# Delta rule output gates: projected with channels on the partitions, applied behind the transposes

## The chip, the core and the metric

The kernel runs on one core of a Trainium2 chip. The metric is the device time of one execution in microseconds; the time of a kernel is the median of its runs. The engines are TensorE (PE, matmuls and weight loads), VectorE (DVE), ScalarE (ACT), GpSimd (POOL) and SyncE (SP, which issues most of the DMAs). Each works through its own queue in order.

## What is computed

One layer of a decoder: a SwiGLU block, a mixer, a second SwiGLU block, a final RMS norm, for 512 tokens of 1024 channels in float32. The mixer has an HGRN2 branch and a gated delta rule branch of 16 value heads. The part at issue is the end of the delta rule branch: its output is normed per head, gated with `silu(gz)`, and projected.

```
proj = (u @ w_in).astype(f32)
(hq, hf, hi, hg, gq, gk, gv, ga, gb, gz, gate_h, gate_g) = jnp.split(proj, offsets, axis=-1)
...
o_g = gated_delta_chunked(q_g, k_g, v_g, beta, g)              # 16 heads of 128 channels
o_g = rmsnorm(o_g, gdn_out_norm) * silu(gz).reshape(B, S, 16, 128)
y_g = o_g.reshape(B, S, 2048) @ w_branch_gdn
y = sigmoid(gate_h) * y_h + sigmoid(gate_g) * y_g
```

## The kernel before

A float32 product is made of three fp32r matmuls: each operand is split into a high part (an ACT cast) and a low part (a DVE difference). `mm3` (L165) issues the three, on lines L166 to L168. A weight slab of 128x512 is loaded by SP into one of 3 `raw` tiles and split into one of 6 `whi` and `wlo` tiles, which are used in turn (`RB`, `WB`). `uh` and `ul` hold the split, normed input with channels on the partitions; the factor of each token's RMS norm is applied to the result, either by `rbc` (along the free axis) or by `rcol` (one per partition).

The mixer is one list schedule written at build time. Every piece of work is a generator that asks for an engine with an estimated duration, for tiles (`get`) and for events (`on`); the class `Desk` runs these in simulated time and so writes the order of all queues. A long line of dense projections (`DENSE`, then sixteen merge gates t0 to t15) is worked through by `product` as a filler between the pieces of the recurrences. In `DENSE`, `k`, `q`, `v` are the delta rule's projections, `y` the first branch's output, and `z0` to `z7` the output gates, each for two heads (a unit `u`).

A `z` projection (L1911 to L1933) has tokens on the partitions: per block of 128 tokens the stationary operand is `uh` or `ul`, and 256 weight columns move, 8 contraction steps of three matmuls for each of 4 token blocks. Two blocks share a PSUM bank (`mm`, 2 banks in all). `gate` (L1619) makes of each 128x256 half `(tanh(z r / 2) + 1) z` with ACT (L1624) and DVE (L1626) in a tile of `gz`; the bank is then given back.

The recurrence of a unit is `g_rec` (L1454). Per chunk, PE makes `pks`, `pw` and `pog`; ACT copies `pw` to `w` (L1465), which `pog` needs. After the last chunk POOL takes the power -1/2 of the mean squares (L1551) and multiplies by `rcol` (L1552); DVE makes the gated output `on` of each 128x128 block, output times `rho` times gate (L1560); PE transposes four blocks into a bank `b` (L1568, `pto`); ACT evicts that with the norm's gain (L1583); SP writes the head to DRAM (`keep`, L1587). For the last unit the transposed output goes straight into the split operand (L1575, L1577).

The close: `tgate` (L1596) multiplies a merge gate by `rbc` (L1601), takes tanh (L1604) and SP writes it out; each holds one of six `ta` tiles until the write has landed, t15 stays on chip. `operand` (L1634) loads a head back into a `ta` tile (`og`, L1643) and splits it (L1649, L1651); heads that go into `uh` and `ul` wait for the end of the projections. `merged` (L1664) loads three tiles for each output tile (`mi`, `mt`, `mg`), of which `mg` holds a `ta` tile. `closing` (L1700) makes the branch products, four slabs of four heads (twelve matmuls) each; the first two products take turns, slab by slab, so the order is first slab of the first, first slab of the second, and so on. A product needs a PSUM bank of the two `mm`, the second one that of t15.

Of the kernel before, what the change touches and what calls it, by code (L numbers as in the profile page):

```python
# [8 lines left out]
F32 = mybir.dt.float32  # L9
# [3 lines left out]
ALU = mybir.AluOpType  # L13
# [19 lines left out]

DENSE = (
# [3 lines left out]
)  # L38
MERGE = (None, None, "a", "a", "b", "b", None, None)
LATE = 1  # L40
# [776 lines left out]
def mixer(tc, mp, e):  # L817
# [636 lines left out]
    def g_rec(u, st):  # L1454
# [84 lines left out]
                D.fire(("s", u, c))  # L1539
        D.put("s")  # L1540
        D.fire(("K", u))
        yield "on", ("norm", u, 1), ("z", u), *[("o", u, c) for c in range(NT)]
        ss, rho, gz = sm[:, 5], sm[:, 6], G["gz"][u % 3]

        yield "use", "DVE", .4
# [4 lines left out]
        yield "use", "POOL", 2.2  # L1550
        pool.tensor_tensor(rho, rho, mhalf[:, :8], op=ALU.pow)  # L1551
        pool.tensor_tensor(v3(rho, 2), v3(rho, 2), mid(rcol, 2), op=ALU.mult)  # L1552
        yield "lag", EASE
        ons = []
        for i in range(2):
            yield "get", "on", 1
            ons.append(places["on"]("on", (P, NT, P)))
            for c in range(NT):
                yield V(200)
                dve.scalar_tensor_tensor(ons[i][:, c], at[i][:, c], rho[:, 4 * i + c:4 * i + c + 1],  # L1560
                                         gz[:, c, i * P:(i + 1) * P], op0=ALU.mult, op1=ALU.mult)
        D.fire(("R", u))
        for i in range(2):
            yield "get", "b", 1
            yield T_(.5)
            pt = ps("pto", "b")
            for c in range(NT):
                pe.transpose(pt[:, c * P:(c + 1) * P], ons[i][:, c], ident)  # L1568
            if u == 7:
                yield "on", "projected"  # L1570
                yield A(560)
                k = 14 + i
                a, b = so[k] = uh[:, k - 8], ul[:, k - 8]
                gn = cs[:, C_GN:C_GN + 1]
                act.activation(a, pt, AF.Copy, scale=gn)  # L1575
                yield V(560)
                dve.scalar_tensor_tensor(b, pt, gn, a.bitcast(F32), op0=ALU.mult, op1=ALU.subtract)  # L1577
                D.put("b")
                D.fire(("so", k))
                continue  # L1580
            og = ons[i].rearrange("p c b -> p (c b)")
            yield A(512)
            act.activation(og, pt, AF.Copy, scale=cs[:, C_GN:C_GN + 1])  # L1583
            D.put("b")
# [11 lines left out]
    def tgate(i, pt):  # L1596

        yield "get", "ta", 1
        yield *V(512), 1
        g = ta("tg")  # L1600
        dve.tensor_tensor(g, pt, rbc, op=ALU.mult)  # L1601
        D.put("mm")
        yield A(512)
        act.activation(g, g, AF.Tanh, scale=0.5)  # L1604
        if i in stay:
            stay[i] = g
            D.fire(("t", i))
# [146 lines left out]
    def more():  # L1754
        yield "on", "branch", ("qm", 1)
        G["kq"].append(ex(0, P, NT, 2, P))
        G["gz"].append(ex(1, P, NT, 256))
# [21 lines left out]
    def weights(k, i):  # L1779
        if k == "B":  # L1780
            return [wn[2 * i + q // 4][:, q % 4 * 512:q % 4 * 512 + 512] for q in range(8)]
        if k == "z":
            return [wn[8 + i][:, q * 512:(q + 1) * 512] for q in range(4)]
        if k == "D":
            return [wab]
        src = wbh[i] if k == "y" else wt[{"Q": 0, "F": 8, "q": 16, "k": 24, "v": 32, "t": 48}[k] + i]
        return [src[:, q * 512:(q + 1) * 512] for q in range(2)]

    def choose():
        under = sum(("f", x) in D.at and x not in D.at for x in convs)  # L1790
        for x in todo:
            k, i = x
            need = {"Q": [("pd", i - 2)] if i > 1 else [], "F": [("L", i - 4)] if i > 3 else [],
                    "B": [("pair", i - 2)] if i > 1 else [], "D": [],
                    "y": [("O", 5), ("S", 6), ("S", 7)], "z": [("R", i - 3)] if i > 2 else [("gz", i) if i < 2 else "more"],
                    "v": [("K", i // 2 - 3)] if i > 5 else [("vb", i) if i < 4 else "more"],
                    "q": [("I", i - 4)] if i > 3 else ["decays" if i < 3 else "more"],
                    "k": [("I", i - 4)] if i > 3 else ["decays" if i < 3 else "more"]}[k]
# [74 lines left out]
    def product():  # L1873
        for n in range(len(todo) + len(gates) + len(line)):
# [22 lines left out]
            if k == "D":  # L1897
# [10 lines left out]
                D.put("w")  # L1908
                D.start((5, n), decays(pt))
                continue  # L1910
            if k == "z":  # L1911
                to = G["gz"][i % 3]
                for t in range(4):
                    if t % 2 == 0:
                        yield "get", "mm", 1
                    for kt in range(KD):
                        if t == 0 and kt % 2 == 0:
                            yield "on", ("slab", (x, kt // 2))
                        yield T_(.36)
                        if t % 2 == kt == 0:  # L1920
                            pt = psd.tile([P, T], F32, tag="mm", name="pnat")
                        hi, lo = made[x, kt // 2]
                        c = slice((kt % 2) * 256, (kt % 2) * 256 + 256)
                        ts = slice(t * P, (t + 1) * P)
                        mm3(pt[:, t % 2 * 256:t % 2 * 256 + 256], uh[:, kt, ts], ul[:, kt, ts], hi[:, c], lo[:, c],
                            kt == 0, kt == KD - 1)
                        if t == 3 and kt % 2:
                            D.put("w")
                    if t % 2:
                        for r in (t - 1, t):  # L1930
                            o = pt[:, r % 2 * 256:r % 2 * 256 + 256]
                            D.start((1, n), gate(x, to, r, o))
                continue  # L1933
            yield "get", "mm", 1
            for q in range(2):
                yield "on", ("slab", (x, q))
# [12 lines left out]
            if k in "qkv":  # L1949
                out = G["vb"][i // 2 % 3 * 2 + i % 2].rearrange("p c b -> p (c b)") if k == "v" else \  # L1950
                    G["kq"][i % 4][:, :, "kq".index(k)]
                th = conv(x, {"q": 0, "k": 8, "v": 16}[k] + i, pt, out, 0 if k == "v" else NT)
            else:
                th = h_q(i, pt) if k == "Q" else h_f(i, pt) if k == "F" else \
                    tgate(i, pt) if k == "t" else branch(i, pt)
# [41 lines left out]
    for i in range(4):  # L1997
        D.start((2, i), h_pair(i))
    for name, tag, n, shape in (("kn", "kn", 3, tb), ("qm", "qm", 2, tb), ("n2", "n2", 2, big),
                                ("gz", "gz", 2, (P, NT, 256)), ("at", "at", 4, tb), ("vb", "vb", 4, tb),  # L2000
                                ("m", "fs", 1, (P, 32, 32)), ("t0", "ft", 1, (P, 32, 8)), ("t12", "ln", 1, (P, 2, 32, 8)), ("x", "x", 1, col),
                                ("we", "we", 1, col), ("w", "w", 1, col)):
        D.start((6, 0), claim(name, tag, n, shape))
# [52 lines left out]
def layout(i):  # L2056
# [20 lines left out]
    wt = np.concatenate([_cols(part[j]) for j in (0, 1, 4, 5, 6, 10, 11)])  # L2077
    vg = np.stack([_pairs(part[j]).reshape(4, P, KD, 256) for j in (2, 3)], 3)
    wn = np.concatenate([vg.reshape(4, P, 2, 2048).transpose(0, 2, 1, 3).reshape(8, P, 2048), _pairs(part[9])])
    wab = np.zeros((D, 64), np.float32)  # L2080
    wab[:, 0:16] = part[7]
    wab[:, 32:48] = part[8]
# [30 lines left out]
```

## Time and profile before

| | |
|---|---|
| median of 3 runs | 1625.3 us (1624.79 to 1625.9) |
| the profiled execution | 1623.19 us, of it span 1621.4 us |
| PE busy | 1599.5 us, 99% of the span |
| DVE, ACT, POOL busy | 1134.0, 858.5, 414.6 us |

The span is the time from the first to the last instruction of the profiled execution. A busy PE counts a matmul from its start to its modelled end; matmuls overlap, so the time that one adds is read from the distance of two starts. The mixer runs from about 340 to 1200 us of the span.

### The profile page before, as it was taken

To read this page: it belongs to the slowest core of one execution; us is meant where nothing else is said; L and a number is where in the kernel's file an instruction comes from. 1 tells how busy PE (TensorE), PEld (TensorE's weight loads), DVE (VectorE), ACT (ScalarE), POOL (GpSimd) and SP (SyncE) were. 2 spreads that over 40 slices of the span, in tenths; PEclk is the share of its full clock that TensorE was granted. 3 is DMA by queue.
4 is the path that set the end of the run, shared out by engine and by line. 5 is a ranking of instruction groups with operands and counts; after the bars stand their busy time and mean duration, and the time that the engine had idled before them with its cause. 6 is when DMAs were issued, how large, how long until landed. Compare 5 with 4: busy or idle time off the path is not lost.

```text
span 1621.4 us, 30263 instructions
## 1 busy us (share of the span) xinstructions
PE 1599.5 (99%) x11170; PEld 1408.9 (87%) x11170; DVE 1134.0 (70%) x2166; ACT 858.5 (53%) x1853; POOL 414.6 (26%) x744
## 2 busy tenths in 40 slices
PE   8999999999999999999999999999999999999997
PEld 7999998887878788888888988888888899999887
DVE  7877774547677778658888888755545877778353
ACT  7766663332434435456566565553325766667232
POOL 0222210101121221254571666510001322220012
PEclk9999999999999999999999999999999999999999
DMA  5988843532312222443323333445545888883343
GB/s 177 236 185 183 183 104 98 172 114 86 104 40 73 88 76 90 129 147 98 102 90 110 104 102 121 150 137 185 159 143 163 192 201 183 184 185 79 115 136 117
DMA packets 128165, 216.52 MB, mean 134 GB/s; under 512 B 21888, under 2 KB 27776, under 8 KB 128016
## 3 DMA queue, kind: packets, MB, share of 16 engines
q1 hardware_dynamic: 110448, 182.89, 35.6%
q0 software_dynamic: 17280, 31.46, 12.8%
q8 instruction: 88, 1.44, 0.4%
q14 instruction: 61, 0.50, 0.1%
q10 hardware_dynamic: 288, 0.22, 0.1%
HBM read 197.45 MB, written 17.07 MB: 132 GB/s over the span
## 4 chain that ended last, share of the span: by engine, by line
PE 92%; DMA 3%; issue 1%; ACT 1%; DVE 1%; POOL 0%; SPq 0%; DVEq 0%; ACTq 0%; POOLq 0%
PE pmm L166 16%; PE pmm L167 15%; PE pmm L168 15%; PE pnat L166 4%; PE pnat L168 4%; PE pnat L167 4%; PE pfa L166 3%; PE pfa L167 3%; PE pfa L168 3%; PE pfx L166 2%; PE pfx L168 2%; PE pfx L167 2%; PE pfy L168 2%; PE pfy L167 2%; PE pfy L166 2%
## 5 line engine op out<-in xcount | busy, mean ns | idle before, releaser
L166 PE MATMUL pmm<-uh,whi 128*128 128x512 f32 x632 | 264.4, 418 | 5.6 <-ACT whi L709 5.6
L1865 ACT CAST whi<-raw 128x512 fp32r<-128x512 f32 x226 | 140.1, 620 | 214.5 <-PE pmm L167 156.8
L1867 DVE TENSOR_TENSOR wlo<-raw,whi 128x512 fp32r<-128x512 f32 x226 | 160.6, 711 | 128.3 <-ACT whi L1865 121.8
L168 PE MATMUL pmm<-uh,wlo 128*128 128x512 f32 x632 | 248.2, 393 | 0.0
L167 PE MATMUL pmm<-ul,whi 128*128 128x512 f32 x632 | 247.9, 392 | 0.0
L420 DVE TENSOR_TENSOR sig<-h,sig 128x1024 fp32r<-128x1024 f32 x80 | 97.7, 1221 | 70.4 <-ACT sig L418 70.4
L166 PEld LDWEIGHTS pmm<-uh,whi 128*128 128x128 f32 x632 | 119.5, 189 | 27.1 <-ACT whi L709 5.6
L168 PEld LDWEIGHTS pmm<-uh,wlo 128*128 128x128 f32 x632 | 119.2, 189 | 26.3
L166 PE MATMUL pmm<-gh,whi 128*128 128x512 f32 (+1 forms) x374 | 140.9, 377 | 0.0
L168 PE MATMUL pmm<-gh,wlo 128*128 128x512 f32 (+1 forms) x374 | 140.9, 377 | 0.0
L167 PE MATMUL pmm<-gl,whi 128*128 128x512 f32 (+1 forms) x374 | 140.8, 377 | 0.0
L167 PEld LDWEIGHTS pmm<-ul,whi 128*128 128x128 f32 x632 | 119.7, 189 | 20.4 <-DVE ul L193 0.2
L418 ACT CAST sig<-h 128x1024 fp32r<-128x1024 f32 x80 | 83.9, 1049 | 88.1 <-PE pfa L168 85.1
L204 POOL TENSOR_TENSOR acc<-acc,sqt 128x512 f32<-128x512 f32 x18 | 24.1, 1338 | 376.4 <-ACT sqt L202 376.3
L166 PE MATMUL pnat<-whi,uh 128*128 128x256 f32 (+1 forms) x328 | 107.7, 328 | 0.0
L162 DVE TENSOR_TENSOR wlo<-raw,whi 128x512 fp32r<-128x512 f32 x74 | 54.9, 746 | 67.6 <-ACT whi L161 66.9
L168 PE MATMUL pnat<-whi,ul 128*128 128x256 f32 (+1 forms) x328 | 100.6, 307 | 0.0
L167 PE MATMUL pnat<-wlo,uh 128*128 128x256 f32 (+1 forms) x328 | 100.4, 306 | 0.0
L395 POOL DMA_DIRECT2D wlo<-w1b x63 | 54.5, 868 | 145.9 <-ACT s L470 101.3
L168 PE MATMUL pfa<-th,sig 128*128 128x256 f32 x320 | 90.9, 284 | 0.6 <-DVE sig L420 0.5
L166 PE MATMUL pfa<-th,sig 128*128 128x256 f32 x320 | 91.0, 284 | 0.4 <-ACT s L475 0.4
L167 PE MATMUL pfa<-tl,sig 128*128 128x256 f32 x320 | 90.7, 283 | 0.0
(489 smaller groups left out, 4566.1 us busy)
## 6 DMA issues: line engine op xcount, KB each, us to landing
raw<-wt SPq DMA_DIRECT2D x128, 256.0 KB
raw<-w1b SPq DMA_DIRECT2D x88, 256.0 KB
raw<-w1a SPq DMA_DIRECT2D x80, 256.0 KB
raw<-wn SPq DMA_DIRECT2D x64, 256.0 KB
wlo<-w1b POOLq DMA_DIRECT2D x63, 256.0 KB, 5.9
wlo<-w1a POOLq DMA_DIRECT2D x57, 256.0 KB, 5.5
raw<-w2b SPq DMA_DIRECT2D x45, 256.0 KB
raw<-w2a SPq DMA_DIRECT2D x40, 256.0 KB
```

The costliest lines, as they stand in the source:

```text
L162: dve.tensor_tensor(lo[:, :f], raw[:, :f], hi[:, :f].bitcast(F32), op=ALU.subtract)
L166: pe.matmul(pt, ah, bh, start=first, stop=False, **kw)
L167: pe.matmul(pt, ah, bl, start=False, stop=False, **kw)
L168: pe.matmul(pt, al, bh, start=False, stop=last, **kw)
L204: add.tensor_tensor(acc, acc, s, op=ALU.add)
L395: pool.dma_start(lo, src_, accum_op=ALU.add)
L418: act.copy(hl[:, 0:2], s)
L420: dve.tensor_tensor(hl[:, 2:4], s, hl[:, 0:2].bitcast(F32), op=ALU.subtract)
L1865: act.copy(hi, raw)
L1867: dve.tensor_tensor(lo, raw, hi.bitcast(F32), op=ALU.subtract)
```

## The change

The gates are now projected like the other dense projections: the weights are stationary, 512 tokens move, one head at a time, so `z0` to `z15` take the place of `z0` to `z7`, in `DENSE` in pairs or singly between the same neighbours. `zgate` multiplies the bank by `rbc` on DVE, which gives the bank back, takes tanh on ACT into a `ta` tile, and makes the product on DVE. The output is scaled by `rho` on ACT, 128x128 at a time, without its gate; after the transposes DVE evicts it with gain and gate in one step. POOL's multiply by `rcol` is gone. For the last unit the operand's two parts are made from that result by an ACT copy and a DVE difference.

```diff
-        yield "on", ("norm", u, 1), ("z", u), *[("o", u, c) for c in range(NT)]
+        yield "on", ("norm", u, 1), *[("o", u, c) for c in range(NT)]
...
         pool.tensor_tensor(rho, rho, mhalf[:, :8], op=ALU.pow)
-        pool.tensor_tensor(v3(rho, 2), v3(rho, 2), mid(rcol, 2), op=ALU.mult)
...
             for c in range(NT):
-                yield V(200)
-                dve.scalar_tensor_tensor(ons[i][:, c], at[i][:, c], rho[:, 4 * i + c:4 * i + c + 1],
-                                         gz[:, c, i * P:(i + 1) * P], op0=ALU.mult, op1=ALU.mult)
+                yield A(128)
+                act.activation(ons[i][:, c], at[i][:, c], AF.Copy, scale=rho[:, 4 * i + c:4 * i + c + 1])
...
+            yield "on", ("z", 2 * u + i)
+            og = ons[i].rearrange("p c b -> p (c b)")
+            yield V(560)
+            dve.scalar_tensor_tensor(og, pt, cs[:, C_GN:C_GN + 1], gz[:, i], op0=ALU.mult, op1=ALU.mult)
+            D.put("b")
...
-            yield A(512)
-            act.activation(og, pt, AF.Copy, scale=cs[:, C_GN:C_GN + 1])
-            D.put("b")
-            D.start((6, u), keep(od[2 * u + i], og, "on", ("od", 2 * u + i)))
+            act.copy(a, og)
+            yield V(512)
+            dve.tensor_tensor(b, og, a.bitcast(F32), op=ALU.subtract)
+            D.fire(("so", k))
...
+    def zgate(i, pt):
+
+        yield "get", "ta", 1
+        yield *V(512), 1
+        z = G["gz"][i // 2 % 3][:, i % 2]
+        dve.tensor_tensor(z, pt, rbc, op=ALU.mult)
+        D.put("mm")
+        yield A(512)
+        th = ta("th")
+        act.activation(th, z, AF.Tanh, scale=0.5)
+        yield V(512)
+        dve.scalar_tensor_tensor(z, th, 1.0, z, op0=ALU.add, op1=ALU.mult)
+        D.put("ta")
+        D.fire(("z", i))
...
-        if k == "z":
-            return [wn[8 + i][:, q * 512:(q + 1) * 512] for q in range(4)]
```

How this stands in the queues, at three places. A row is line, operation, output, inputs and size; `pnat` and `pmm` are banks of projections, `pto` of transposed outputs, `on` a head's output, `gat` its place before the norm, `ggz` its gate.

PE, inside a gate projection, before:

```order
L166 MATMUL pnat_8995<-whi_8717,uh_71 128x256
L167 MATMUL pnat_8995<-wlo_8716,uh_71 128x256
L168 MATMUL pnat_8995<-whi_8717,ul_72 128x256
L166 MATMUL pnat_8995<-whi_8788,uh_71 128x256
L167 MATMUL pnat_8995<-wlo_8787,uh_71 128x256
L168 MATMUL pnat_8995<-whi_8788,ul_72 128x256
L1568 MATMUL pto_9018<-sq_76,on_8884 128x128 x4
```

and now:

```order
L166 MATMUL pmm_8797<-uh_71,whi_8576 128x512
L167 MATMUL pmm_8797<-ul_72,whi_8576 128x512
L168 MATMUL pmm_8797<-uh_71,wlo_8575 128x512
L1566 MATMUL pto_8806<-sq_76,on_8721 128x128 x4
L1433 MATMUL pq3_8817<-h_70,gn2_7364 64x64 x8
L166 MATMUL pmm_8797<-uh_71,whi_8576 128x512
```

The weights have become the stationary operand and the moving one is twice as wide; in the whole program PE has 384 matmuls of 512 columns where it had 768 of 256, and no other matmul is added or removed.

The outputs of the first unit, on DVE before:

```order
L1218 TENSOR_TENSOR ci_8928<-pmm_8816,rbc_74 128x512
L1867 TENSOR_TENSOR wlo_8913<-raw_8729,whi_8914 128x512
L1560 SCALAR_TENSOR_TENSOR on_8884<-gat_6223,sm_7073,ggz_6568 128x128 x3
L1867 TENSOR_TENSOR wlo_8955<-raw_8826,whi_8956 128x512
L1560 SCALAR_TENSOR_TENSOR on_8884<-gat_6223,sm_7073,ggz_6568 128x128
L1560 SCALAR_TENSOR_TENSOR on_8974<-gat_6224,sm_7073,ggz_6568 128x128 x4
```

and now on ACT:

```order
L1267 COPY x4_7942<-ptk_8678 128x512
L1559 ACTIVATE on_8645<-gat_6223,sm_7073 128x128 x3
L1877 CAST whi_8713<-raw_8585 128x512
L1559 ACTIVATE on_8645<-gat_6223,sm_7073 128x128
L1559 ACTIVATE on_8721<-gat_6224,sm_7073 128x128 x4
L1423 COPY h_70<-pq2_8684 32x8x32
```

The eight scalings have moved from DVE to ACT, where they share the queue with weight casts and the recurrence's copies; the gate comes in behind the transposes, on DVE.

ACT at the close, around the cast of the last head that is loaded back (`og_13593` before, `og_13184` now), before:

```order
L1865 CAST whi_13604<-raw_13532 128x512
L1575 ACTIVATE uh_71<-pto_13613,cs_75 128x512
L1865 CAST whi_13630<-raw_13558 128x512
L1649 CAST uh_71<-og_13593 128x512
L1865 CAST whi_13649<-raw_13580 128x512
```

and now:

```order
L1663 CAST uh_71<-og_13110 128x512
L1663 CAST uh_71<-og_13119 128x512
L1877 CAST whi_13190<-raw_13127 128x512
L1877 CAST whi_13208<-raw_13143 128x512
L1877 CAST whi_13226<-raw_13170 128x512
L1663 CAST uh_71<-og_13184 128x512
L1877 CAST whi_13246<-raw_13193 128x512
```

Counting the slabs of the closing products from one in PE's order, `whi_13630` is the eleventh and `whi_13226` the twelfth; with six tiles in turn they follow the fifth (third slab of the first product) and the sixth (third slab of the second). SP at the same place, now (before, the write of t13's gate, `tg`, stood ahead of the nine loads):

```order
L1589 DMA td_3951<-tg_12917 128x512
L1841 DMA raw_12941<-wbg 128x512
L1684 DMA mi_12946<-md_3950 128x512
...
L1692 DMA mg_12993<-td_3951 128x512
L1841 DMA raw_13000<-wbg 128x512
L1589 DMA td_3951<-tg_12990 128x512
```

`tg_12917` is t12's gate and `tg_12990` t13's: the write of t13 has moved behind the loads for `merged`.

## Rows read from the trace of the kernel before

**Rows 1.** The page, parts 1 and 2: busy us and clock.

```profile
PE 1599.5 (99%) x11170; PEld 1408.9 (87%) x11170; DVE 1134.0 (70%) x2166; ACT 858.5 (53%) x1853; POOL 414.6 (26%) x744
...
PEclk9999999999999999999999999999999999999999
```

**Rows 2.** Busy by stage: sum, then PE, PEld, DVE, ACT, POOL, clock, DMA.

```profile
780.00:800.00 20.00, 20.00 (x148) 19.05 (x147) 17.63 (x42) 11.73 (x30) 15.43 (x38) 1.00 0.35 104
...
1120.00:1140.00 20.00, 19.09 (x89) 15.46 (x88) 13.34 (x26) 8.78 (x15) 1.15 (x2) 1.00 0.69 232
```

**Rows 3.** Waits of PE: us in total, times, longest.

```profile
PE pmm L166 <- DVE tg L1601: 0.9, 1, 0.9
```

**Rows 4.** Groups by line and form: busy us, mean ns, idle before.

```profile
L166 PE MATMUL pnat<-whi,uh 128*128 128x256 f32 x256 | 77.8, 304 | 0.0
```

**Rows 5.** Timeline of PE: start us, us, what.

```profile
764.01 0.47 PE L166 MATMUL pmm<-uh,whi 128*128 128x512 f32 x1
764.32 0.39 PE L167 MATMUL pmm<-ul,whi 128*128 128x512 f32 x1
764.55 0.40 PE L168 MATMUL pmm<-uh,wlo 128*128 128x512 f32 x1
...
776.40 0.39 PE L166 MATMUL pmm<-uh,whi 128*128 128x512 f32 x1
...
779.13 0.28 PE L166 MATMUL pnat<-whi,uh 128*128 128x256 f32 x1
...
780.55 0.36 PE L166 MATMUL pnat<-whi,uh 128*128 128x256 f32 x1
780.75 0.28 PE L167 MATMUL pnat<-wlo,uh 128*128 128x256 f32 x1
...
795.18 0.28 PE L166 MATMUL pnat<-whi,uh 128*128 128x256 f32 x1
...
796.25 0.40 PE L166 MATMUL pmm<-uh,whi 128*128 128x512 f32 x1
```

**Rows 6.** Single lines: ns min/median/max, first and last start.

```profile
L1626 DVE SCALAR_TENSOR_TENSOR ggz<-thg,pnat x24: 406/420/422, 652.4 to 1040.9; 128x256 f32<-128x256 f32 x24
L1560 DVE SCALAR_TENSOR_TENSOR on<-x,sm,ggz x16: 343/346/348, 926.2 to 1133.7; 128x128 f32<-128x128 f32 x16
L1218 DVE TENSOR_TENSOR ci<-pmm,rbc x32: 672/691/693, 607.0 to 1018.7; 128x512 f32<-128x512 f32 x32
L1577 DVE SCALAR_TENSOR_TENSOR ul<-pto,cs,uh x2: 751/752/752, 1136.7 to 1139.9; 128x512 fp32r<-128x512 f32 x2
L1583 ACT ACTIVATE on<-pto,cs x14: 677/687/691, 780.8 to 1090.9; 128x512 f32<-128x512 f32 x14
L1471 ACT COPY gat<-pog x32: 242/265/273, 733.7 to 1018.7; 128x128 f32<-128x128 f32 x32
L1252 ACT ACTIVATE gat<-gb,gx x32: 386/390/416, 567.1 to 855.6; 128x128 f32<-128x128 f32 x32
```

**Rows 7.** Timelines at the close, by engine: SP, DVE, PE, ACT.

```profile
1116.43 0.42 SPq L1670 DMA_DIRECT2D mi<-md  x1
...
1123.15 0.32 SPq L1590 DMA_DIRECT2D td<-tg  x1
...
1128.33 0.69 DVE L1601 TENSOR_TENSOR tg<-pmm,rbc 128x512 f32<-128x512 f32 x1 [1.72 <-DMA td<-tg]
...
1142.34 0.68 DVE L1651 TENSOR_TENSOR ul<-og,uh 128x512 fp32r<-128x512 f32 x1
...
1129.07 0.50 PE L166 MATMUL pmm<-sogb,whi 128*128 128x512 f32 x1 [0.91 <-DVE tg L1601]
...
1143.78 0.39 PE L166 MATMUL pmm<-uh,whi 128*128 128x512 f32 x1
...
1141.08 0.62 ACT L1865 CAST whi<-raw 128x512 fp32r<-128x512 f32 x1 [1.20 <-PE pmm L167]
1141.60 0.61 ACT L1649 CAST uh<-og 128x512 fp32r<-128x512 f32 x1
```

More of the change, by code (lines that the diff above doesn't have):

```diff
@@ L1549, in g_rec @@
         yield "lag", EASE
-        yield "use", "POOL", 2.2
+        yield "use", "POOL", 1.8
         pool.tensor_tensor(rho, rho, mhalf[:, :8], op=ALU.pow)
-        pool.tensor_tensor(v3(rho, 2), v3(rho, 2), mid(rcol, 2), op=ALU.mult)
         yield "lag", EASE
@@ L1568, in g_rec @@
                 pe.transpose(pt[:, c * P:(c + 1) * P], ons[i][:, c], ident)
[L1569 to L1577, printed above, removed]
-                D.put("b")
-                D.fire(("so", k))
+            yield "on", ("z", 2 * u + i)
[3 more added lines that the diff above has]
+            D.put("b")
+            if i == 1:
+                D.fire(("Z", u))
+            if u < 7:
+                D.start((6, u), keep(od[2 * u + i], og, "on", ("od", 2 * u + i)))
                 continue
-            og = ons[i].rearrange("p c b -> p (c b)")
+            yield "on", "projected"
             yield A(512)
-            act.activation(og, pt, AF.Copy, scale=cs[:, C_GN:C_GN + 1])
-            D.put("b")
-            D.start((6, u), keep(od[2 * u + i], og, "on", ("od", 2 * u + i)))
+            k = 14 + i
+            a, b = so[k] = uh[:, k - 8], ul[:, k - 8]
+            act.copy(a, og)
+            yield V(512)
+            dve.tensor_tensor(b, og, a.bitcast(F32), op=ALU.subtract)
+            D.fire(("so", k))
     def keep(to, tile_, tag, event=None):
@@ L1756, in more @@
         G["kq"].append(ex(0, P, NT, 2, P))
-        G["gz"].append(ex(1, P, NT, 256))
+        G["gz"].append(ex(1, P, 2, T))
         for n, i in (("at", 2), ("vb", 3)):
@@ L1781, in weights @@
             return [wn[2 * i + q // 4][:, q % 4 * 512:q % 4 * 512 + 512] for q in range(8)]
-        if k == "z":
-            return [wn[8 + i][:, q * 512:(q + 1) * 512] for q in range(4)]
         if k == "D":
             return [wab]
-        src = wbh[i] if k == "y" else wt[{"Q": 0, "F": 8, "q": 16, "k": 24, "v": 32, "t": 48}[k] + i]
+        src = wbh[i] if k == "y" else wt[{"Q": 0, "F": 8, "q": 16, "k": 24, "v": 32, "t": 48, "z": 64}[k] + i]
         return [src[:, q * 512:(q + 1) * 512] for q in range(2)]
@@ L1794, in choose @@
                     "B": [("pair", i - 2)] if i > 1 else [], "D": [],
-                    "y": [("O", 5), ("S", 6), ("S", 7)], "z": [("R", i - 3)] if i > 2 else [("gz", i) if i < 2 else "more"],
+                    "y": [("O", 5), ("S", 6), ("S", 7)], "z": [("Z", i // 2 - 3)] if i > 5 else [("gz", i // 2) if i < 4 else "more"],
                     "v": [("K", i // 2 - 3)] if i > 5 else [("vb", i) if i < 4 else "more"],
@@ L1910, in product @@
                 continue
[L1911 to L1933, printed above, removed]
             yield "get", "mm", 1
@@ L1954, in product @@
                 th = h_q(i, pt) if k == "Q" else h_f(i, pt) if k == "F" else \
-                    tgate(i, pt) if k == "t" else branch(i, pt)
+                    tgate(i, pt) if k == "t" else zgate(i, pt) if k == "z" else branch(i, pt)
             D.start((3, 8, n) if k in "qk" else (5, n), th)
@@ L1999, in mixer @@
     for name, tag, n, shape in (("kn", "kn", 3, tb), ("qm", "qm", 2, tb), ("n2", "n2", 2, big),
-                                ("gz", "gz", 2, (P, NT, 256)), ("at", "at", 4, tb), ("vb", "vb", 4, tb),
+                                ("gz", "gz", 2, (P, 2, T)), ("at", "at", 4, tb), ("vb", "vb", 4, tb),
                                 ("m", "fs", 1, (P, 32, 32)), ("t0", "ft", 1, (P, 32, 8)), ("t12", "ln", 1, (P, 2, 32, 8)), ("x", "x", 1, col),
@@ L2076, in layout @@
     part = [w_in[:, off[j]:off[j + 1]] for j in range(12)]
-    wt = np.concatenate([_cols(part[j]) for j in (0, 1, 4, 5, 6, 10, 11)])
+    wt = np.concatenate([_cols(part[j]) for j in (0, 1, 4, 5, 6, 10, 11, 9)])
     vg = np.stack([_pairs(part[j]).reshape(4, P, KD, 256) for j in (2, 3)], 3)
-    wn = np.concatenate([vg.reshape(4, P, 2, 2048).transpose(0, 2, 1, 3).reshape(8, P, 2048), _pairs(part[9])])
+    wn = vg.reshape(4, P, 2, 2048).transpose(0, 2, 1, 3).reshape(8, P, 2048)
     wab = np.zeros((D, 64), np.float32)
```

4 rows, old and new, of the table DENSE are left out of this document.

## The prediction

> **What bounds the kernel now.** I read the page's busy shares first, then the table by stage, the waits of TensorE, its timeline inside one gate projection, and last the end of the mixer, where its longest mixer wait lies. TensorE (PE) is busy 99% of the span, the other engines 70% at most, and the granted clock reads 9 tenths or more in all 40 slices, the 2.4 GHz level throughout [rows 1]. By stage, PE is busy 20.00 of 20 us in the middle of the mixer; of the forty windows of 20 us from 380 to 1180 us only two show less; the second is 1120 to 1140 [rows 2]. PE's waits name one of note late in the mixer: 0.9 us for the eviction of a merge gate [rows 3]. So in this stage time changes only if PE is given less to stream, or if a new wait opens. VectorE (DVE) is busy 17.63 of those 20 us, ScalarE (ACT) 11.73: neither sets the time, but DVE has little room.
>
> **The change part by part.** *The gate projection, PE.* Before, 8 projections run 96 matmuls each with 256 columns moving: the group row counts 256 for one of the three lines, 768 in all [rows 4]. After, 16 projections run 24 each with 512 columns moving: 384. Pitch by the timeline: nine 256-column matmuls take from 795.18 to 796.25, 1.07/9 = 0.119 us; twelve 512-column ones from 776.40 to 779.13, 2.73/12 = 0.2275 us [rows 5]. The sum: 768 x 0.119 = 91.3 us against 384 x 0.2275 = 87.4 us, **3.9 us less**, all of it on the path, since PE does not idle here. Lower bound: soon after a piece of other work a 512-column matmul takes 764.32 to 764.55, 0.23, which gives 91.4 - 88.3 = 3.1 us. I take 3.9, from long unbroken runs of both widths. Interruptions cost the same in both: after a foreign piece the first dense matmul takes 764.01 to 764.32, 0.08 longer than its pitch, with 512 columns, and 780.55 to 780.75, 0.08 longer, with 256 [rows 5]; the order has 241 returns to dense work where there were 249, and where two foreign pieces now follow each other they pay each other, so I count 0; at most it is 8 x 0.08 = 0.6 us gained, the upper bound 4.5.
>
> The rule that speaks against this gain: the Trainium skill, page "TensorE: Matmul & The Clock Gate", section "Wait — 56ns, not 53.3ns?", gives start-to-start as the columns at 2.4 GHz plus about 2.5 ns for each matmul, whatever its width. By it two 256-column matmuls would cost only 2.5 ns more than one of 512, and the sum would be 384 x 2.5 ns = 1.0 us. The trace does not agree: it shows 10 ns for each pair.
>
> *DVE.* Out: 32 gate multiplies of 0.420 us and 64 output multiplies of 128x128 at 0.346 [rows 6], 35.6 us. In: 16 evictions by the row norm like the convolution's 0.691, 16 products in SBUF I put at the same 0.69, 16 gated evictions from PSUM like 0.752, and two differences for the last unit in place of two of 0.752 [rows 6]: 34 us. It is about even and covered by PE; if DVE ran late, PE would meet it at the banks below.
> *ACT.* Out: 32 half-width tanh, and 14 evictions at 0.687 [rows 6]. In: 16 full tanh, which do the same elements, and 64 copies of 128x128 with a scale column. No such copy is in the trace; the nearest rows are 0.265 (a plain copy of that size out of PSUM) and 0.390 (an activation of that size with a column operand) [rows 6]: 17 to 25 us, so ACT gains some 7 to 15 us of 858, under PE's cover. GpSimd loses 8 tiny multiplies.
> *Where the copies wait.* They now stand on ACT behind GpSimd's power, where DVE's multiplies stood. Behind them on ACT are the weight casts, which run up to six slabs ahead of PE, and copies of the recurrence, for one of which PE has some eight matmuls, 1.8 us, in hand. I count 0, from 0 to 1.3 us a unit (below).
> *The projection's bank* is given back after one multiply by the row norm (0.69) instead of after a tanh and a product per half: PE needs it again a whole projection, 5.5 us, later, in both. 0 us. The gate tile borrows one of the six `ta` tiles; 0.
>
> *The end of the mixer.* Here the order moves two waits. First, the **tile of gate t15**. Before, five of the six `ta` tiles were held, so t15's multiply waited for t14's write: issued at 1123.15, it let DVE go on at 1128.33, 5.2 us later, and PE lost 0.9 us at 1129.07 [rows 3, 7]. After, nine merge loads stand on SP ahead of t13's write, not behind it, and t14's tanh stands on ACT behind a weight cast that waits for the first half of t15's projection, and five copies. Counting from the end of t13's projection: that cast 8.2 (36 x 0.2275), the cast and copies 0.6 + 5 x some 0.3 (between the 0.265 and 0.390 above), tanh 0.6 like a cast: t14's write leaves at about 10.8. The second branch product, which needs t15's bank, is due after 48 matmuls, one transpose group and 12 matmuls: 10.9 + 0.4 + 2.7 = 14.1. If the write lands as late as the row's 5.2, DVE is done at 16.7 and PE waits 2.7; in a queue that has drained it is less, down to a wait of 0. The first of the nine loads went out at 1116.43, 6.7 us before the write [rows 7]; by the order it goes out some 13 us before it now (about 2 us ahead of the end of t13's projection), so I take a value near the lower end, **0.5**.
> Second, the **last reloaded head**, which the fourth weight slab of the first product uses in its second group of three. Its ACT cast stood behind the cast of `whi_13630`, which takes the buffer of the first product's third slab; now it stands behind `whi_13226`, which takes the buffer of the *second* product's third slab, one slab later. Before: that cast at 1141.08, the head's at 1141.60, its low part on DVE at 1142.34 + 0.68 = 1143.02; the product reached it at 1143.78 + 0.68 = 1144.46, 1.4 us to spare [rows 7]. After, the weight cast cannot begin before the fourth slab starts, the same chain takes 1.94 us from there and PE asks at 0.68: **1.3 us waited**. It is 1.0 if PE waits for each part by itself, since one matmul with the high part then gets through. Together 0.5 + 1.3 - 0.9 = **0.9 us more** (bounds -0.9, should both vanish, and 2.7 + 1.3 - 0.9 = +3.1).
>
> **Sum.** On the profiled execution: 1623.2 - 3.9 + 0.9 = 1620.2 us. The median of the runs lies 2.1 us above that execution; so 1625.3 - 3.0 = **1622.3 us**, 0.18% less. About 0.2%, 3.25 us, is what a measurement of this kernel can tell from no change (1622.05), so this sits almost on that line.
>
> **The rivals.** *B, the closing waits go.* If t14's write lands in time and the last head's cast is not held by the buffer ring, the old 0.9 goes too: 1625.3 - 3.9 - 0.9 = 1620.5. For it: the loads have drained by then. Against: the position of the cast is fixed by the order.
> *C, the closing slips.* t14's write takes its 5.2 us, and everything behind it on DVE slips: +3.1, so 1625.3 - 0.8 = 1624.5. For it: DVE is in order, and the casts of the two heads held until the projections end stand right behind t15.
> *D, slower: copies ahead of the copy that PE waits for.* Eight copies in a row take 8 x 0.265 to 8 x 0.390 = 2.1 to 3.1 us on ACT. Where the recurrence's `w` copy (between the `pw` and `pog` matmuls) stands right behind them, PE has 1.8 us in hand and loses up to 1.3. In all 8 units: +10.4, 1632.7. It decides from 0.4 us a unit. Against: in the order the `w` copy stands that close in one unit only.
> *E, the width brings nothing.* If the 10 ns by which a pair of 256-column matmuls exceeds one of 512 came from where the unbroken runs lie and not from the width, the gain would be 0: 1625.3 + 0.9 = 1626.2. The rows speak against it: the two runs lie within 20 us of each other, at one clock. The rule of the Trainium skill's page "TensorE: Matmul & The Clock Gate" named above goes most of this way; by it 1.0 us is left, 1625.2.
>
> **How the numbers follow.** The forecast's case has 0.50 and spreads over 1620.9 to 1623.7, half of it on either side of the line; B 0.20, faster; C 0.17 and E 0.03, within 0.2%; D 0.10, slower. Faster: 0.25 + 0.20 = 0.45; same 0.25 + 0.17 + 0.03 = 0.45; slower 0.10. The range leaves out D, the outermost part of B and a little of E: 1619.5 to 1626.0.
>
> **What would show it.** In the changed profile: PE's matmul count lower by 384 and gate projections at 0.2275 us pitch; PE 20.00 of 20 us in the mixer's windows up to the close; at the close a wait of PE for t15's multiply of about 0.5, and one of about 1.3 for the DVE low part of the last reloaded head. B shows neither; C shows the first above 2; D shows PE waiting for the `w` copy in many units. Wrong I would be if the 512-column pitch among so many interruptions were nearer 0.23 or above, or if PE waited for transposes of outputs that ACT has not scaled yet.

## The result, and the profile after

The changed kernel takes 1630.07 us (median of 11 runs, 1625.84 to 1634.14), the kernel before 1625.72 (11 runs beside it): a ratio of 1.0027, 95% interval 1.0018 to 1.0036. It is slower by 4.4 us; the forecast was 1622.3, the range ended at 1626.0, and slower had a chance of 0.10. Its profiled execution has a span of 1629.8 us.

The page after, parts 1 and 2, answers to [rows 1]; below it two windows of 20 us, with the columns of [rows 2]:

```profile
PE 1602.3 (98%) x10786; PEld 1391.3 (85%) x10786; DVE 1132.6 (69%) x2118; ACT 863.3 (53%) x1887; POOL 417.4 (26%) x736
...
PEclk9999999999999999999999999999999999999998
```

```profile
720.00:740.00 20.00, 17.83 (x107) 14.41 (x108) 12.74 (x29) 13.46 (x43) 17.10 (x40) 0.91 0.22 71
...
1120.00:1140.00 20.00, 16.94 (x68) 13.47 (x67) 9.23 (x16) 8.06 (x18) 0.00 (x0) 0.83 0.59 204
```

PE has the 384 matmuls less that were forecast. But in the window from 720 us it is busy 17.83 us at a mean granted clock of 0.91, in the one from 1120 us 16.94 at 0.83, where before it was busy 20.00 and 19.09 at 1.00 (the second of these stands in [rows 2], the first here):

```profile
720.00:740.00 20.00, 20.00 (x139) 17.12 (x138) 14.18 (x33) 14.02 (x45) 17.18 (x39) 1.00 0.36 106
```

The prediction had named 20.00 of 20 us in every window up to the close as its sign. The page's clock line, in 40 slices, is too coarse to show either place. PE's waits name both. Those of the changed kernel in the mixer (compare [rows 3]), and in a fence of its own the second one of the kernel before, which is late in the first branch:

```profile
PE pmm L166 <- DVE tg L1600: 3.1, 1, 3.1
PE ptk L1264 <- DVE ci L1217: 2.9, 1, 2.9
...
PE pmm L166 <- ACT uh L1663: 0.4, 1, 0.4
...
PE pmm L167 <- DVE ul L1665: 0.3, 1, 0.3
```

```profile
PE ptv L1372 <- DVE gqm L1316: 0.4, 1, 0.4
```

The first row is the multiply of gate t15 (L1601 before), 3.1 us in place of 0.9. The last two belong to the last reloaded head. The second is new and was in no step of the prediction.

**The new wait at 719 us.** `ptk` are the transposes of a key or query (L1264); they need a convolution's output on DVE, that needs ACT, and ACT stands. ACT's timeline, after, and the same instruction before:

```profile
720.47 0.40 ACT L1252 ACTIVATE x<-gb,gx 128x128 f32<-128x128 f32 x1 [4.90 <-DMA gb<-gtd]
```

```profile
717.21 0.99 ACT L1252 ACTIVATE x<-gb,gx 128x128 f32<-128x128 f32 x3 [1.70 <-DMA gb<-gtd]
```

`gb` is the spread-out decay row of a head, loaded by SP. SP's timeline, after, then before:

```profile
707.56 0.42 SPq L1589 DMA_DIRECT2D md<-yh  x1
...
711.32 0.38 SPq L1834 DMA_DIRECT2D raw<-wt  x1
711.74 0.42 SPq L1247 DMA_DIRECT2D gb<-gtd  x1
```

```profile
710.66 0.43 SPq L1247 DMA_DIRECT2D gb<-gtd  x1
711.19 0.38 SPq L1590 DMA_DIRECT2D md<-yh  x1
```

Two transfers of 256 KB that stood behind `gb` now stand ahead of it: the write of the last `y` projection (`md`, ahead of four loads for the neighbours `gfs` too), and a weight load (`raw`). `gb` is issued 1.1 us later and is there 8.7 us after its issue (711.74 to 720.47), not 6.5 (710.66 to 717.21). ACT's queue is in order, so the convolution's tanh behind it (L1229) is late, and PE is. PE's timeline, after:

```profile
718.86 0.39 PE L168 MATMUL pmm<-uh,wlo 128*128 128x512 f32 x1
722.17 0.66 PE L1264 MATMUL ptk<-sq,h 128*128 128x128 f32 x4 [2.92 <-DVE ci L1217]
722.58 0.57 PE L166 MATMUL pmm<-uh,whi 128*128 128x512 f32 x1
...
726.40 0.68 PE L1433 MATMUL pq<-gut,gn 64*64 64x64 f32 x16
```

The distance 718.86 to 722.17 is 3.31 us, 3.1 beyond the pitch. Behind it nine matmuls take from 722.58 to 726.40, 0.42 each, where 0.2275 is usual [rows 5]: the 1.2 GHz level. That is 1.8 us more by this pitch; a run below (E2) has the same nine at the 2.4 GHz level, where they and the step to the next piece take 2.25 us (723.55 to 725.80), and against that it is 1.6. Together **4.9 us**, or 4.7 by E2's stretch.

**The close.** SP's, DVE's and PE's timelines, after; before stands in [rows 7]:

```profile
1120.84 0.38 SPq L1589 DMA_DIRECT2D td<-tg  x1
...
1129.19 0.38 SPq L1589 DMA_DIRECT2D td<-tg  x1
```

```profile
1116.43 0.69 DVE L1600 TENSOR_TENSOR tg<-pmm,rbc 128x512 f32<-128x512 f32 x1 [0.90 <-PE pmm L168]
...
1126.25 0.69 DVE L1600 TENSOR_TENSOR tg<-pmm,rbc 128x512 f32<-128x512 f32 x1 [3.26 <-DMA td<-tg]
...
1132.77 0.69 DVE L1600 TENSOR_TENSOR tg<-pmm,rbc 128x512 f32<-128x512 f32 x1 [4.03 <-DMA td<-tg]
```

```profile
1130.07 0.39 PE L168 MATMUL pmm<-soat,wlo 128*128 128x512 f32 x1
1133.52 0.80 PE L166 MATMUL pmm<-sogb,whi 128*128 128x512 f32 x1 [3.06 <-DVE tg L1600]
...
1138.81 0.81 PE L1566 MATMUL pto<-sq,on 128*128 128x128 f32 x4
```

The three multiplies are those of t13, t14 and t15. t13's write leaves at 1120.84, behind the nine loads for `merged` (before: ahead of them, and t14's leaves at 1123.15). So t14's multiply waits 3.26 us for t13's tile. t14's write leaves at 1129.19 (why so late is taken up below), and t15's multiply waits 4.03 us for that. PE stands 3.45 - 0.23 = 3.2 us beyond its pitch, and the twelve matmuls behind take 5.29 us (1133.52 to 1138.81) for 12 x 0.2275 = 2.73: 2.6 more. Together **5.8 us**, where the kernel before lost 0.9. The last reloaded head costs two waits more.

Whether these parts are causes, and what the change is worth without them, the experiments had to show.

### The profile page after: what moved, and what is told of

It reads as the page before. It is cut to its first block, busy times and chain, and to the rows that moved or that the text cites. A ratio compares the mean times of both kernels' runs of the same rounds, so it can differ in the third digit from the quotient of the medians.

```text
span 1629.8 us, 29469 instructions
## 1 busy us (share of the span) xinstructions
PE 1602.3 (98%) x10786; PEld 1391.3 (85%) x10786; DVE 1132.6 (69%) x2118; ACT 863.3 (53%) x1887; POOL 417.4 (26%) x736
## 5 line engine op out<-in xcount | busy, mean ns | idle before, releaser
L166 PE MATMUL pmm<-uh,whi 128*128 128x512 f32 x760 | 319.9, 421 | 5.9 <-ACT whi L709 5.5
L168 PE MATMUL pmm<-uh,wlo 128*128 128x512 f32 x760 | 299.1, 393 | 0.0
L167 PE MATMUL pmm<-ul,whi 128*128 128x512 f32 x760 | 298.3, 393 | 0.3 <-DVE ul L1665 0.3
L1877 ACT CAST whi<-raw 128x512 fp32r<-128x512 f32 x226 | 140.3, 621 | 233.5 <-PE pmm L167 184.8
L166 PEld LDWEIGHTS pmm<-uh,whi 128*128 128x128 f32 x760 | 143.9, 189 | 32.3 <-ACT whi L709 5.5
L168 PEld LDWEIGHTS pmm<-uh,wlo 128*128 128x128 f32 x760 | 143.4, 189 | 32.1
L167 PEld LDWEIGHTS pmm<-ul,whi 128*128 128x128 f32 x760 | 144.0, 190 | 25.3 <-DVE ul L1665 0.6
L161 ACT CAST whi<-raw 128x512 fp32r<-128x512 f32 x74 | 43.9, 594 | 84.5 <-PE pmm L167 77.0
L386 ACT ACTIVATE wlo<-raw 128x512 fp32r<-128x512 f32 x120 | 75.1, 626 | 24.9 <-PE pfa L168 14.6
L395 POOL DMA_DIRECT2D wlo<-w1a x57 | 49.4, 867 | 134.3 <-ACT s L470 96.2
```

Source lines behind the costliest of these rows:

```text
L161: act.copy(hi[:, :f], raw[:, :f])
L166: pe.matmul(pt, ah, bh, start=first, stop=False, **kw)
L167: pe.matmul(pt, ah, bl, start=False, stop=False, **kw)
L168: pe.matmul(pt, al, bh, start=False, stop=last, **kw)
L386: act.activation(lo, raw, AF.Copy, scale=-1.0)
L395: pool.dma_start(lo, src_, accum_op=ALU.add)
```

## The experiments

All ratios are to the kernel before, run on the same chip in the same rounds. All kernels compute the whole layer. An edit moves the line numbers of its kernel a little (the gate multiply, L1600, is L1605 in the first run).

**E1: only SyncE's order around `gb` as before.** The write of `y7` and the weight load are held until `gb` has been issued.

```diff
-        sp.dma_start(to, tile_)
+        if event == ("y", 7):
+            held.append(lambda: sp.dma_start(to, tile_))
+        else:
+            sp.dma_start(to, tile_)
...
             sp.dma_start(gb, gtd[hd_:hd_ + 1].rearrange("o (c b) -> o c b", c=NT).to_broadcast([P, NT, P]))
+            while held:
+                held.pop(0)()
...
-                sp.dma_start(raw, src)
+                if held:
+                    held.append(lambda raw=raw, src=src: sp.dma_start(raw, src))
+                else:
+                    sp.dma_start(raw, src)
```

> The changed kernel with one thing moved on SyncE: the write of the eighth y projection and one weight load, which stand ahead of a load of gb at 711.7 us of its span, go behind it, as in the kernel before; every other queue keeps its order. Theory (order of transfers): the 512 KB that stood ahead of the neighbour loads and of gb made gb land 8.7 us after its issue where the kernel before saw about 6.5, ScalarE waited 4.9 us for it, TensorE 2.9 us behind that and then ran nine matmuls at 0.43 us instead of 0.23 (1.8 us): the wait falls below 0.5, its slow matmuls with it, so 4.5 us less: about 1625.5 us. Rival (the load is late for itself, by other traffic or by chance of the profiled execution): the wait of 2 to 3 us stays, or was not in the median at all, and the time stays at 1630 within 1 us.

Measured: 1626.34 us, ratio 0.9999 (0.9990 to 1.0008): about 4.5 us less than the change. ACT's row for `gb`, issued at 710.94:

```profile
717.19 0.40 ACT L1254 ACTIVATE x<-gb,gx 128x128 f32<-128x128 f32 x1 [1.39 <-DMA gb<-gtd]
```

6.25 us after its issue, and PE's list of waits no longer has `ptk`. The order of two transfers was worth all of it; the rival is out. The closing wait stayed (3.5 us there).

**E2: seven tiles in turn in place of six.**

```diff
-    ta = alloc("ta", TA)
+    ta = alloc("ta", TA + 1)
...
-        e["nextnorm"](C_F2, e["h2"], late=True, tag="ta", bufs=TA)(d, mp)
+        e["nextnorm"](C_F2, e["h2"], late=True, tag="ta", bufs=TA + 1)(d, mp)
```

> The changed kernel with seven tiles of the kind ta in memory in place of six; the order of every queue is as in the changed kernel, only the waits for a tile to come free are shorter. Theory (chain of two tiles at the close): gate t14 waited 3.26 us for the write of t13, which stands behind nine loads, and t15 then 4.03 us for the write of t14, and TensorE 3.06 us for t15, with twelve slow matmuls behind (2.4 us): with a tile more neither waits for a write, the TensorE wait goes, and the time falls by 5 to 5.5 us to about 1625. The two waits of 0.3 to 0.6 us for the last reloaded head stay. Rival (VectorE and ScalarE are late for other reasons, such as a cast that waits for its weight load): t15 still comes 1 us or more late and at least 3 us of loss stay, 1628 or above.

Measured: 1630.40 us, ratio 1.0021 (1.0013 to 1.0030). The closing wait is gone from PE's list, as expected, and yet the time is that of the change. **E3: E1 and E2 together.**

> Both edits together: gb's load ahead of the write and the weight load, and seven tiles. Theory: the two losses lie 400 us apart and add up, so 1630.1 - 4.5 - 5.3 = about 1620.3 us, and what is left against the kernel before is the narrower stream (3.9 us less), the old closing wait (0.9 less) and the last head (1.1 more), which gives 1625.7 - 3.9 - 0.9 + 1.1 = 1622.0. Rival (the wider matmuls bring nothing): 1625.5 or above.

Measured: 1626.30 us, 0.9998 (0.9989 to 1.0007), no better than E1 alone. **E4: E3, and the cast of the last reloaded head one place earlier on ScalarE.**

```diff
+        if key == (("m", 2), 3):
+            yield "on", ("so", 13)
+        if key in ((("m", 3), 0), (("m", 3), 1), (("m", 3), 2)):
+            yield "on", ("slab", (("m", 2), 3))
```

> Both edits of the third run, and the cast of the last reloaded head stands on ScalarE ahead of the twelfth weight cast of the closing products, not behind it (its low part on VectorE likewise). Theory: the two waits of TensorE for that head (0.53 and 0.58 us beyond the pitch in the changed kernel) vanish: 1.1 us less than the third run, about 1620.9. Rival (the head is late because its load lands late): TensorE waits as long as before or longer for it, or for the weight slab whose cast now stands behind, and the time is that of the third run.

Measured: 1624.80 us, 0.9992 (0.9983 to 1.0001). Its two waits are gone, and 1.5 us by the medians, though the intervals of E3 and E4 overlap. But now PE waits nowhere in the mixer, and the kernel is barely ahead of the one before. Either the wider stream brings nothing (rival E), or E2 had cost something. The windows of the final projection, far behind the gates, told which. First the changed kernel, then E2, columns as in [rows 2]:

```profile
1240.00:1260.00 20.00, 20.00 (x90) 16.54 (x89) 10.36 (x15) 10.12 (x17) 5.17 (x4) 1.00 0.55 183
```

```profile
1240.00:1260.00 20.00, 20.00 (x87) 16.09 (x86) 9.93 (x14) 10.89 (x19) 5.18 (x4) 1.00 0.53 168
```

The same matmuls, PE never idle, the clock at 1.00 in both: 90 of them in 20 us, and 87. The timelines there, again the changed kernel, then E2; 17 starts lie between the two rows of each:

```profile
1245.02 0.39 PE L167 MATMUL pmm<-m,whi 128*128 128x512 f32 x1
...
1248.87 0.39 PE L166 MATMUL pmm<-m,whi 128*128 128x512 f32 x1
```

```profile
1244.93 0.39 PE L167 MATMUL pmm<-m,whi 128*128 128x512 f32 x1
...
1248.90 0.40 PE L166 MATMUL pmm<-m,whi 128*128 128x512 f32 x1
```

3.85/17 = 0.2265 us, and 3.97/17 = 0.2335. A seventh tile of 2176 bytes (17 x 128) had moved every tile that is laid out behind it. In E2, matmuls whose moving operand moved (`m`, the first eight heads, the first branch's outputs) start 0.233 us apart, those with `uh`, which did not move, 0.227 to 0.229 as before. E2 to E4 had put a new cost in the place of the one they removed.

**E5: E4 with the additional tile at the end of the pool.** t14 alone uses it, six tiles are used in turn again, and no other tile moves.

```diff
-        g = ta("tg")
+        g = mp.tile([P, T], F32, name="tg14") if i == 14 else ta("tg")
```

> The edits of the fourth run, but the additional tile is one of its own for gate t14, at the end of the pool, so that no other tile changes its address; every queue keeps the order of the fourth run. Theory (addresses): in the runs with seven tiles in turn everything behind them moved by 2176 bytes, and matmuls whose moving operand moved start 0.233 us apart where they start 0.2267 apart in the changed kernel (192 of the final projection, 192 of the y projections, 192 of the closing products with the first eight heads, and some of the first branch: about 600 x 6.5 ns = 3.9 us); uh, which did not move, keeps 0.2270. With the old addresses the time falls by 3.9 us from 1624.8 to 1620.9. Rival (the wider stream brings nothing and the pitch has another cause): the time stays at 1624.8 within 1 us and the 0.233 stays.

Measured: **1620.06 us** (5 runs, 1617.88 to 1623.25), ratio 0.9960 (0.9947 to 0.9973), 6.5 us ahead of the kernel before, and ahead of the changed one too. Against E4, from which it differs only in where that tile lies, it is 5.2 us less by the ratios. The windows that answer to the two of the changed kernel:

```profile
720.00:740.00 20.00, 20.00 (x153) 16.22 (x152) 14.35 (x34) 14.65 (x47) 17.10 (x40) 1.00 0.31 96
1120.00:1140.00 20.00, 20.00 (x94) 16.55 (x93) 12.43 (x19) 10.99 (x23) 0.00 (x0) 1.00 0.67 220
```

**E6: the changed kernel with only that tile.** The edit is that of E5, with six tiles in turn and none of the other edits.

> The changed kernel with only the tile of its own for gate t14 at the end of the pool; the wait for gb and that for the last head stay. Theory: the closing wait of 3.06 us and the slow matmuls behind it (2.4 us) go, nothing else changes: 1630.1 - 5.4 = 1624.7, up to 1626 if the slow clock is not met in every execution. Rival (the closing wait is not in the median, since the second run showed none of it gone): 1629 to 1630.

Measured: 1625.83 us, 0.9993 (0.9984 to 1.0002): some 5.5 us less than the change. DVE's rows for t14 and t15 carry no wait:

```profile
1122.10 0.68 DVE L1600 TENSOR_TENSOR tg<-pmm,rbc 128x512 f32<-128x512 f32 x1
...
1126.51 0.69 DVE L1600 TENSOR_TENSOR tg<-pmm,rbc 128x512 f32<-128x512 f32 x1
```

The wait for `gb` is still there (3.07 us), and the two for the head. But t14's write is still late, though nothing holds t14's multiply now; t13's multiply starts at 1115.62 there, and on SP:

```profile
1127.66 0.33 SPq L1589 DMA_DIRECT2D td<-tg  x1
```

**E7 and E8: the kernel before, moved by 128 and by 256 bytes.** An unused tile at the start of the mixer's pool, of 32 and of 64 columns, cleared once on DVE; nothing else.

```diff
+    dve.memset(mp.tile([P, 32], F32, name="pad"), 0.0)
     lm = mp.tile([P, 8, 8], F32, name="lm")
```

> The kernel before with an unused tile of 128 bytes at the start of the mixer's pool; nothing else differs and no queue changes. Theory (addresses): a moving operand of 512 float32 that starts 128 bytes off a multiple of 256 costs 6.5 ns a matmul; all of the mixer's tiles move by 128 bytes, so about 600 matmuls pay: 1626.0 + 3.9 = 1629.9, pitch of the final projection 0.233. Rival (in the second run something else slowed them, such as which tiles lie next to each other): 1626.0 and 0.2267.

> The same with 256 bytes. Theory (addresses, in steps of 256): the time of the kernel before, 1626.0, and a pitch of 0.2267. Rival (any shift costs, or the added instruction does): as the run with 128 bytes, 1629.9.

Measured: 128 bytes 1629.86 us, 1.0021 (1.0012 to 1.0030); 256 bytes 1626.59, 0.9994 (0.9985 to 1.0003). Windows of E7, then E8:

```profile
1240.00:1260.00 20.00, 20.00 (x87) 16.08 (x86) 10.00 (x14) 8.61 (x14) 4.58 (x4) 1.00 0.51 165
```

```profile
1240.00:1260.00 20.00, 20.00 (x90) 16.58 (x89) 9.84 (x14) 9.36 (x16) 4.05 (x4) 1.00 0.52 163
```

The pitch follows the address, not the presence of a tile. The kernel before and the changed one both have 90 matmuls in this window, so this is no part of the change's loss.

**E9: the kernel before, with only SyncE's order around `gb` of the changed one.** The reverse of E1, in the same way: the neighbour loads, `gln` and `gb` are held.

```diff
-            sp.dma_start(gb, gtd[hd_:hd_ + 1].rearrange("o (c b) -> o c b", c=NT).to_broadcast([P, NT, P]))
+            f = lambda gb=gb, hd_=hd_: sp.dma_start(
+                gb, gtd[hd_:hd_ + 1].rearrange("o (c b) -> o c b", c=NT).to_broadcast([P, NT, P]))
+            held.append(f) if hd_ == 4 else f()
...
         sp.dma_start(to, tile_)
+        if event == ("y", 7):
+            while len(held) > 1:
+                held.pop(0)()
...
                 sp.dma_start(raw, src)
+                if len(held) == 1:
+                    held.pop()()
```

> The kernel before, with SyncE's order around one load of gb as in the changed kernel: the write of the eighth y projection ahead of the four neighbour loads, one weight load ahead of gb; no other queue changes, the gates are projected as before. Theory (order of transfers): gb lands 2 to 3 us later behind these 512 KB, TensorE, which had 0.3 us to spare there, waits 2 to 3 us at the transposes of the next unit and in part of the executions runs at the lower clock for some matmuls behind (0 to 1.8 us): 1626.5 + 2.5 to 4.5 = 1629 to 1631. Rival (the changed kernel lost this time through its own projections or scalings, not through the order of transfers): 1626.5, no wait above 0.5 us there.

Measured: 1628.66 us, 1.0014 (1.0005 to 1.0023). ACT's row for `gb`, issued at 713.38, and PE's:

```profile
720.98 0.99 ACT L1254 ACTIVATE x<-gb,gx 128x128 f32<-128x128 f32 x3 [3.69 <-DMA gb<-gtd]
```

```profile
723.26 0.66 PE L1266 MATMUL ptk<-sq,h 128*128 128x128 f32 x4 [1.61 <-DVE ci L1217]
```

7.6 us after its issue, PE waits 1.6: the order alone makes the wait, without any gate changed, but only half of it (1.6 us, not 2.9). The size was overestimated. The missing part lies in the landing, 7.6 us where the changed kernel has 8.7, behind the same kinds of transfers in the same order; why, stays open. Nor is the whole 2.3 us of E9 this wait: in its profile the two old waits of PE are longer too, 1.7 us at the close for 0.9 and 1.0 at `ptv` for 0.4. E8, in which no queue changed its order, has 1.5 at `ptv`, so waits of this kind differ by about 1 us between executions.

**E10: the kernel before, with only t13's write behind the nine loads.**

```diff
-        sp.dma_start(to, tile_)
+        f = lambda: sp.dma_start(to, tile_)
+        held.append(f) if event == ("t", 13) else f()
...
             sp.dma_start(g, td[8 + d])
+            if d == 2:
+                held.pop()()
```

> The kernel before with one thing moved on SyncE: the write of gate t13 goes behind the nine loads for the merges, as in the changed kernel. Theory (chain of two tiles): the write leaves at about 1121.4 us, not 1116.1, lands some 5 us later, t14's multiply waits for that until 1126.5, its write leaves at 1128, lands 3.5 to 5 us later, t15's multiply waits for it, and TensorE waits 3.5 to 5.5 us at the second branch product where it waited 0.9, with up to 2.4 us of slow matmuls behind: 1626.5 + 2.6 to 6.5 = 1629 to 1633. Rival (the changed kernel's closing wait comes from its ScalarE copies and late casts): the wait stays below 1.5 us and the time at 1626.5.

Measured: 1628.97 us, 1.0016 (1.0007 to 1.0024). DVE's row for t14, and PE's:

```profile
1127.81 0.69 DVE L1602 TENSOR_TENSOR tg<-pmm,rbc 128x512 f32<-128x512 f32 x1 [5.97 <-DMA td<-tg]
```

```profile
1128.56 0.50 PE L166 MATMUL pmm<-sogb,whi 128*128 128x512 f32 x1 [2.44 <-DVE tg L1602]
...
1129.82 0.63 PE L167 MATMUL pmm<-soat,whi 128*128 128x512 f32 x1
1130.25 0.63 PE L168 MATMUL pmm<-soat,wlo 128*128 128x512 f32 x1
```

The write alone makes a closing wait, and the time is at the low end of what was expected. But it is another wait than I had said: DVE waits 5.97 us with t14's multiply, PE 2.44 for t14's bank, at the first branch product, and t15 comes in time. So this run makes the first link of the chain, t14 waiting for t13's write, and not the second.

**E11: E5 with the scalings of the outputs on VectorE.**

```diff
-                act.activation(ons[i][:, c], at[i][:, c], AF.Copy, scale=rho[:, 4 * i + c:4 * i + c + 1])
+                dve.tensor_scalar(ons[i][:, c], at[i][:, c], rho[:, 4 * i + c:4 * i + c + 1], None, op0=ALU.mult)
```

> The kernel of the fifth run with the 64 scalings of the outputs on VectorE in place of ScalarE, at the same places in the program. Theory (either engine has room, since TensorE sets the time and no wait of it names these scalings): the time of the fifth run, 1620.1, within 1 us. Rival (the scaling on ScalarE holds up copies on which TensorE waits): 1 us or more faster, 1619 or below. A second rival (VectorE, busy some 17.6 of 20 us in these windows, has no room for 64 more operations): 1 to 5 us slower, 1621 to 1625.

Measured: 1620.29 us, 0.9969 (0.9959 to 0.9979). The intervals of E5 and E11 overlap and the medians lie 0.2 us apart (1.5 by the ratios): which engine scales makes no difference that can be told here.

## Why the prediction was wrong

**The gate projection (3.9 us less): right in mechanism, near in size.** The mixer's length on PE, from the last matmul of the first SwiGLU block to the first of the second, before, after, and in E5:

```profile
238.25 0.28 PE L168 MATMUL pfx<-uh,sig 128*128 128x256 f32 x1
...
1269.85 0.28 PE L166 MATMUL pfa<-uh,whi 128*128 128x256 f32 x1
```

```profile
239.16 0.28 PE L168 MATMUL pfx<-uh,sig 128*128 128x256 f32 x1
...
1277.70 0.28 PE L166 MATMUL pfa<-uh,whi 128*128 128x256 f32 x1
```

```profile
242.67 0.28 PE L168 MATMUL pfx<-uh,sig 128*128 128x256 f32 x1
...
1269.18 0.28 PE L166 MATMUL pfa<-uh,whi 128*128 128x256 f32 x1
```

1031.60, 1038.54 and 1026.51 us. (E5's mixer starts 4.4 us later than the kernel before's; its profiled execution is the slowest of its five, 1623.25 us, and loses that time in the first block, where the code is the same.) E5 has no wait of PE in it, the kernel before the 0.9 and 0.4 above; without these it would be 1030.3, so the narrower count of matmuls gives 1030.3 - 1026.5 = 3.8 us. (Taken by the distance of starts the two old waits cost 1.07 and 0.60, and 3.4 are left.) The lower bound of 3.1 held, rival E is out. By the rule of the Trainium skill, page "TensorE: Matmul & The Clock Gate", section "Wait — 56ns, not 53.3ns?", an estimate would have left 1.0 us; the measurement, 3.4 to 3.8, decides against it here.

**VectorE, ScalarE, the copies on ScalarE (0 on the path): right.** ScalarE's copies take 0.391 us each, the upper of the two bounds. By the page of the profile DVE has 1.4 us less, ACT 4.8 more, below the 7 to 15 forecast. No wait of PE names `pog`, so rival D, the only one on the slower side, had the sign by luck: its mechanism did not happen, and E11 says the same.

**The tile of t15 (0.5 us, bounds 0 to 2.7): the mis-sized term.** The step that failed is "t14's write leaves at about 10.8". Counted from t13's multiply at 1116.43, it left 12.8 us later. Two things made it late. ACT, after, the weight cast ahead of t14's tanh, and that tanh:

```profile
1125.59 0.62 ACT L1877 CAST whi<-raw 128x512 fp32r<-128x512 f32 x1 [2.44 <-DMA raw<-wbg]
...
1127.60 0.62 ACT L1603 ACTIVATE tg<-tg 128x512 f32<-128x512 f32 x1
```

I had this cast wait for PE, until 8.2; it waited for its own weight load, until 9.2. That part has nothing to do with tiles: in E6, where t14's multiply waits for nothing, t14's write still leaves 12.0 us after t13's multiply (1115.62 to 1127.66). The other 0.7 us is a chain that I had left out. I had moved t13's write behind nine loads, but let only t15 wait for a write; t14's own multiply needs a tile too, and with five of six held it waits for t13's. Its tanh is not late by that, since the multiply is done at 1126.94. But behind the multiply on DVE stands the low part of a weight slab (1128.06), SP's next weight load waits for that (1128.77, in E6 1126.39), and t14's write stands behind this load. The rest of the step was about right: the second branch product was due at 1130.3 (14.1 forecast after t13, 13.9 seen), and t14's write landed in some 3.5 us, less than the 5.2 of the row before. With 12.0 in place of 12.8 and the rest as seen, PE would still have waited some 2.5 us, by an estimate from these numbers, so the cast is the larger part. E6 takes the wait for t14's write away, by giving t15 another tile; no run brings the weight load forward.

**The last reloaded head (1.3 us): right.** PE's wait rows give 0.4 + 0.3, the distances of its starts 1.1 beyond the pitch, and E4 took the waits away by moving the cast.

**What was in no term: the load of `gb`.** I compared the orders where the change works, and on SP only at the close. At 707 to 712 us SP's order had moved as well, in the stretch of the `y` projections, and the profile before showed that it was tight: ACT was already waiting 1.70 us for that load. E1 takes the wait away, E9 makes 1.6 us of it.

**What was in no price: the clock behind a wait.** I wrote that PE ran at the 2.4 GHz level throughout and priced each wait at its own length. Behind the two waits of the changed kernel it ran on at the 1.2 GHz level for a while, some 1.7 and 2.6 us more.

The sum with the measured terms, on the profiled mixer, by distances of starts: the 3.4 less for the stream, 1.7 less for the old waits, 4.9 for `gb`, 5.8 for the close, 1.1 for the head: +6.7, where the mixer is 6.9 longer. The rest of that span's difference, 1.5 us, lies outside the mixer, in code that is the same. By the ratios to the kernel before (times 1626 us) E1 gives 4.5 us, E6 5.5 and E4 against E3 1.0, 11.0 together, and E5 against the change 10.9: the parts add up, each to within 1.5 us or so. Rival C came closest in mechanism, a late write of t14, but at 1624.5 it stopped at the upper bound of the same wrong step.

## What to carry to other kernels

Where a scheduler writes the queues, any edit moves transfers far from itself: compare the DMA queue's order over the whole program and look first where an engine was already waiting for a load in the profile before. Follow a chain of borrowed tiles link by link, since each write that is moved is waited for by the very next borrower, and ask of each cast on the way whether its load has landed, not only whether its buffer is free. And an added buffer is only a clean repair if it leaves the other tiles where they were; when a fix removes a wait and the time stays, read the pitch in a stretch that it should not have touched.

## What the runs showed of the hardware

**The address of the moving operand.** 128x512 float32 matmuls in three fp32r parts start 0.2265 us apart with the operand on its old address or 256 bytes on, and 0.2335 us with it 128 bytes on (E2, E7, E8): 3% at an unchanged clock, 3.4 us for the kernel before in E7. Only shifts of 128, 2176 and 256 bytes were tried.

**The clock after a wait is not the same each time.** In E10 matmuls ran at the 1.2 GHz level behind a wait of 2.44 us; in E2 none did behind one of 2.78:

```profile
723.13 0.66 PE L1264 MATMUL ptk<-sq,h 128*128 128x128 f32 x4 [2.78 <-DVE ci L1217]
...
723.86 0.39 PE L167 MATMUL pmm<-ul,whi 128*128 128x512 f32 x1
724.09 0.40 PE L168 MATMUL pmm<-uh,wlo 128*128 128x512 f32 x1
```

So a wait of this size can cost its own length or nearly twice that. That may be why the runs of the changed kernel spread over 8.3 us and those of the kernel before, beside it, over 5.0; it was not tried by itself.
